# Turning the attention values around from the tile their projection writes, instead of from a copy that went through DRAM

## The chip, the core and the metric

The kernel runs on one core of a Trainium2 chip. The metric is the device time of one execution in microseconds (us); lower is better. A core has a matrix engine (TensorE, PE in the rows), a vector engine (VectorE, DVE), an activation engine (ScalarE, ACT), GpSimd (POOL) and SyncE (SP), which only issues transfers. Each engine works through its own list of instructions in order and waits on semaphores for the others. SBUF is the on-chip memory, PSUM the accumulators that TensorE writes.

## The reference, cut to what matters

One decoder layer over 1024 tokens of width 1024. All branches start from one projection of the normalised input:

```python
proj = h @ w_in
xa, za, q, k, v, zb, qi, ki, wi, ga, gb = jnp.split(proj, IN_SPLITS, axis=-1)
ya = s5_mixer(xa, ...)                       # state space branch, gated by za
yb = dsa_mixer(q, k, v, qi, ki, wi)          # 8 heads, one shared key/value head of width 64
merged = sigmoid(ga) * ya + sigmoid(gb) * (yb * silu(zb)) @ w_b_o
```

`dsa_mixer` scores all keys with an indexer, keeps 256 per query, and attends over them with softmax: `o = p @ v`, with `v` of 1024 x 64. To multiply by `v`, TensorE wants tokens on the partitions (the 128 rows of SBUF), while the projection delivers `v` with its 64 columns on the partitions and the tokens along the row. So `v` has to be transposed once.

## The kernel before

The kernel is one long program for a scheduling library: it says what depends on what and in which pool a tile lives, and the library fixes each engine's order and the semaphores. A pool of n buffers gives a new tile a buffer when the last user of an old one is done.

The projections are made in column blocks of 128 (`project`): the weights are loaded by SP, split into a high and a low part (ACT casts, DVE subtracts), and TensorE makes three products per pair of tiles (`three`, lines 137 to 139). The results go to PSUM banks that rotate among three (`dense_bank`) and are read out by ACT and DVE into tiles of the pool `stage`, which has three buffers of 128 x 1024 (`staged`). These three buffers serve many names one after the other: the raw values `vraw`, the gates `gas`, `gbs`, `zbs` on their way to DRAM, the eight blocks `wg` of the modulation weights that DVE sums into `gsum`, the query tile `qt0`, and the copy `vt` of the values.

In order of the program: the indexer's scores; the search for the top 256 (DVE counts); the state space branch (names `y`, `hs`, `mk`), woven together with the projections of q, k and v (`kv`), then of the gates `ga` (8 blocks), the first two blocks of `gb` and the four of `zb`. Then two products with `gsum` (`gate`, line 737), the transposes of `v` (line 754), and `flag_ps` (line 829), a 1 x 1 product that says whether the search succeeded. DVE casts it to an integer (`rows_ok`, line 831), loads it into a register and branches (line 833): with success it skips the slow exact search. Then attention begins: scores `l` (line 894), DVE adds the bias and finds the maximum (line 897), ACT takes the exponential (line 908), DVE divides (line 912), TensorE transposes (`pt`, line 919) and multiplies by `v_s` (lines 938 and 939). The remaining six `gb` blocks and other dense products are strewn between these by a table of numbers (`pace`, `leads`), so that TensorE has work while DVE and ACT make the softmax.

The values before: `with_v` copies rows 64 to 127 of the projection `kv` into `vraw`; ACT's queue stores them to `vd` in DRAM; much later SP loads `vd` into partitions 0 to 63 of a fresh staged tile `vt`, and TensorE transposes that in eight pieces into one PSUM bank, `v_ps`. `split` (lines 77 and 78) makes the high part of `v_s` on ACT and the low part on DVE. The PSUM pools of attention (`psl` and others) take over the banks that `ps_a.close()` gives back before the attention stage; the bank of `v_ps` and that of `flag_ps` are among them.

```python
def staged(name, dtype=F32, shape=(128, L)):
    return stage.tile(list(shape), dtype, name=name, tag="sg")
```

Of the kernel before, what the change touches and what calls it, by code (L numbers as in the profile page):

```python
# [9 lines left out]
F32 = mybir.dt.float32  # L10
F32R = mybir.dt.float32r
# [9 lines left out]
L = 1024  # L21
NT = L // 128
# [12 lines left out]
def tile_hybrid(ctx, tc, x, c, norm_g, w_mod, b_mod, w_in, a_re, a_im, b_re, b_im,  # L35
                c_re, c_im, d_skip, log_dt, w_glu, b_glu, w_a_o, w_b_o, w_out,
                final_g, out):
    nc = tc.nc
# [5 lines left out]
    def f32(ap):  # L44
        return ap.bitcast(F32)
# [8 lines left out]
    spill = ctx.enter_context(tc.tile_pool(name="spill", bufs=1, space=DRAM))  # L54

    def bank(name):
        return ps1.tile([128, 512], F32, name=name, tag="b1")
# [10 lines left out]
    ident = const.tile([128, 128], F32, name="ident")  # L68
# [4 lines left out]
    def staged(name, dtype=F32, shape=(128, L)):  # L73
        return stage.tile(list(shape), dtype, name=name, tag="sg")

    def split(src, hi, lo, hi_eng=None, lo_eng=None):
        (hi_eng or nc.scalar.copy)(hi, src)  # L77
        (lo_eng or nc.vector).tensor_sub(lo, src, f32(hi))  # L78
# [71 lines left out]
    def project(src, c0, m, rh, rl, nkt, name, early=True, pieces=(0, 1), rows=None):  # L150

        wh, wl = load_w(src, c0, m, nkt, name, early, rows)
        for j in pieces:
            sl = slice(512 * j, 512 * j + 512)
            ps = dense_bank(f"{name}_ps")
            for kt in range(nkt):
                three(ps[:m], wh[:, kt], wl[:, kt], rh[kt][:, sl], rl[kt][:, sl],
                      kt == 0, kt == nkt - 1)
            yield ps[:m], sl
# [2 lines left out]
    yds = []  # L162
    qd = spill.tile([8, 128, L], F32, name="qd")
    kd = spill.tile([2, 128, L], F32, name="kd")
    vd = spill.tile([64, L], F32, name="vd")
    zad = spill.tile([4, 128, L], F32, name="zad")
    zbd = spill.tile([4, 128, L], F32, name="zbd")
    gad = spill.tile([ND, 128, L], F32, name="gad")
# [5 lines left out]
    with ExitStack() as st:  # L174
# [32 lines left out]
        ps = bank("rows_ps")  # L207
# [92 lines left out]
    kpool = att.enter_context(tc.tile_pool(name="kpool", bufs=1, side="right"))  # L300
# [19 lines left out]
    def stack_k(parts, dst_h, dst_l, name):  # L320
        hi, lo = hi_lo(parts, name, 64)
        for o in (0, 64):
            nc.scalar.dma_start(f32(dst_h[o:o + 64]), hi[0:64])
            nc.scalar.dma_start(f32(dst_l[o:o + 64]), lo[0:64])
# [16 lines left out]
    with ExitStack() as st:  # L341
# [11 lines left out]
        for nm, src in (("ar", a_re), ("ai", a_im)):  # L353
# [4 lines left out]
            ps = bank(nm + "_ps")  # L358
# [100 lines left out]
        ps = bank("wi_ps")  # L459
# [5 lines left out]
        for i in groups[0] + groups[1]:  # L465
            w = 128 * (i + 1)
            for h in range(8):
                for o, n in chunks(w):
                    ps = bank(f"s{i}_{h}_{o}")
# [55 lines left out]
    for dst, e0, e1, nm in ((cx, c_re, c_im, "cxr"), (cy, c_im, c_re, "cyr")):  # L525
# [3 lines left out]
        ps = bank(nm + "_ps")  # L529
# [6 lines left out]
    ps = bank("dsk_ps")  # L536
# [47 lines left out]
    for m in range(4):  # L584
# [3 lines left out]
        for half in range(2):  # L588
# [23 lines left out]
            ps = bank(f"mt{q}_ps")  # L612
# [6 lines left out]
            ps = bank(f"k{q}_ps")  # L619
# [15 lines left out]
            ps = bank(f"s{q}_ps")  # L635
# [37 lines left out]
            ps = bank(f"y{q}_ps")  # L673
# [15 lines left out]
    ps = bank("rows2_ps")  # L689
# [6 lines left out]
    t = staged("vraw")  # L696

    def with_v(parts):
        for ps, sl in parts:
            nc.scalar.copy(t[64:128, sl], ps[64:128])  # L700
            yield ps, sl

    stack_k(with_v(project(w_in, K, 128, h_hi, h_lo, ND, "kv")), kd[0], kd[1], "k")
    nc.scalar.dma_start(vd, t[64:128])

    def gates(c0, ms, dst, silu, name):

# [11 lines left out]
    for kt in range(ND):  # L719
        t = staged(f"wg{kt}")  # L720
# [13 lines left out]
    for j in range(2):  # L734
        ps = bank(f"gate{j}")
# [10 lines left out]
    nc.sync.dma_start(f32(att_k), kd.rearrange("e p n -> p e n"))  # L746
    att_q = staged("qt0", F32R, (128, 8, 128))
    nc.sync.dma_start(f32(att_q), qd[:, :, 0:128].rearrange("h p n -> p h n"))
    att_v = kpool.tile([128, NT, 128], F32R, name="v_s")
    vt = staged("vt")  # L750
    nc.sync.dma_start(vt[0:64], vd)
    ps = bank("v_ps")
    for j in range(NT):
        nc.tensor.transpose(ps[:, 64 * j:64 * j + 64], vt[0:64, 128 * j:128 * j + 128], ident[:64, :64])
    split(ps.rearrange("p (j d) -> p j d", j=NT), att_v[:, :, 0:64], att_v[:, :, 64:128])


    for i in range(2):
# [5 lines left out]
    def scr(name, dtype=F32, n=6):  # L764
        return sepool.tile([128, n], dtype, name=name)
# [38 lines left out]
    for g, tiles in enumerate(groups):  # L804
        for n, i in enumerate(tiles):
# [7 lines left out]
            j = sepool.tile([128, L], F32, name=f"j{i}", tag="cf", bufs=2)[:, :w]  # L813
# [19 lines left out]
    with tc.If(found < 6 * 128):  # L833
# [4 lines left out]
        thr, d, cnt, need = scr("thr", I32), scr("d", I32), scr("cntb"), scr("need")  # L838
# [196 lines left out]
    for k, (m, pieces) in enumerate(steps):  # L1035
# [8 lines left out]
        t = wpool.tile([128, D], F32, name=f"wo{k}", tag="wraw")  # L1044
# [7 lines left out]
    for t in range(NT):  # L1052
# [6 lines left out]
        for n, (o, w) in enumerate(pieces):  # L1059
            sl = slice(o, o + w)  # L1060
            ps = pso.tile([128, 512], F32, name=f"o{t}_ps", tag="o")
# [48 lines left out]
```

## Time and profile before

| what | value |
|---|---|
| device time, median of 3 runs | 911.64 us (910.56 to 913.61) |
| time of the profiled execution | 913.2 us |
| its span, first to last instruction | 911.4 us |
| mean granted clock of TensorE | 0.975 of full |
| TensorE busy | 853.0 us, 94% of the span |
| VectorE busy | 655.6 us, 72% |
| ScalarE busy | 406.5 us, 45% |

The profiled execution is 1.8 us longer than its span; a change of the span is a change of the time. [...]

### The profile page before, as it was taken

How to read it: one execution, taken by the hardware profiler on the slowest of the kernel's cores; microseconds unless marked ns; L12 is line 12 of the kernel's file. 1: busy time of each engine (PE TensorE's matmuls, PEld its weight loads, DVE VectorE, ACT ScalarE, POOL GpSimd, SP SyncE). 2: the span in 40 equal slices, each digit the busy share in tenths (PEclk: the TensorE clock that was granted, in tenths of full speed). 3: DMA queues.
4: the chain of work that ended last, by engine and by line, in shares of the span. 5: the costliest groups of instructions: out<-in, count | busy, mean ns of one | idle time of the engine just before them, and what ended most of it. 6: DMA issues, size and time to landing. Idle time of an engine off the chain costs nothing.

```text
span 911.4 us, 12005 instructions
## 1 busy us (share of the span) xinstructions
PE 853.0 (94%) x4105; PEld 703.9 (77%) x4105; DVE 655.6 (72%) x1381; ACT 406.5 (45%) x803; POOL 138.2 (15%) x244
## 2 busy tenths in 40 slices
PE   4999999989889998999769999999999999999996
PEld 4887788877668877888558888887888888777885
DVE  5665898498989894687226677668987786956753
ACT  7553576354355542332225564457555443432311
POOL 0000100079446943000000000000000000221000
PEclk9799999999999998999969999999999999999999
DMA  9925611463443332573423323135314323644331
GB/s 328 315 65 131 147 49 47 74 181 89 121 117 119 110 111 65 183 263 92 116 70 97 92 83 112 47 105 151 103 47 129 92 81 93 198 150 149 139 131 54
DMA packets 124388, 110.38 MB, mean 121 GB/s; under 512 B 20954, under 2 KB 108066, under 8 KB 124324
## 3 DMA queue, kind: packets, MB, share of 16 engines
q1 hardware_dynamic: 96386, 77.46, 28.3%
q10 hardware_dynamic: 27938, 32.13, 12.0%
q8 instruction: 32, 0.52, 0.2%
q14 instruction: 32, 0.26, 0.1%
HBM read 76.67 MB, written 26.48 MB: 113 GB/s over the span
## 4 chain that ended last, share of the span: by engine, by line
PE 52%; DVE 13%; issue 4%; DMA 4%; ACT 2%; ACTq 2%; POOL 0%; DVEq 0%; SPq 0%
PE l L894 4%; DVE cj L770 3%; PE gb_ps L137 3%; PE gb_ps L138 3%; PE gb_ps L139 3%; PE pt L919 3%; PE o_ps L139 3%; PE o_ps L138 3%; PE o_ps L137 3%; PE pv L939 2%; PE pv L938 2%; PE ao_ps L139 2%; PE ao_ps L137 2%; PE ao_ps L138 2%; PE zb_ps L138 2%
## 5 line engine op out<-in xcount | busy, mean ns | idle before, releaser
L78 POOL TENSOR_TENSOR wo_l<-wo,wo_h 128x1024 fp32r<-128x1024 f32 x5 | 12.2, 2447 | 459.0 <-ACT wo_h L77 429.8
L770 DVE TENSOR_SCALAR_CACHE_REDUCE cj<-score,mid 128x1024 bf16<-128x1024 f32 (+2 forms) x72 | 67.6, 939 | 14.2 <-ACT mid L793 8.8
L897 DVE CUSTOM_DVE_ANT_0 S<-l,bias 128x384 f32<-128x384 f32 (+5 forms) x96 | 52.6, 553 | 26.5 <-PE l L894 23.4
L908 ACT ACTIVATE S<-S,stt 128x128 f32<-128x128 f32 (+7 forms) x64 | 49.1, 770 | 40.1 <-DVE stt L905 39.9
L77 ACT CAST ph<-pt 128x512 fp32r<-128x512 f32 x72 | 41.3, 584 | 43.4 <-PE pt L919 38.4
L78 DVE TENSOR_TENSOR pl<-pt,ph 128x512 fp32r<-128x512 f32 x72 | 48.8, 686 | 9.1 <-ACT ph L77 8.7
L894 PE MATMUL l<-k_s,qt 128*128 128x384 f32 (+5 forms) x192 | 50.2, 349 | 4.9 <-issue 4.9
L138 PE MATMUL gb_ps<-h_lo,gb_wh 128*128 128x512 f32 x128 | 51.4, 402 | 0.0
L137 PE MATMUL gb_ps<-h_hi,gb_wh 128*128 128x512 f32 x128 | 51.4, 401 | 0.0
L138 PE MATMUL o_ps<-wo_l,m_hi 128*128 128x512 f32 (+1 forms) x136 | 51.3, 378 | 0.0
L139 PE MATMUL o_ps<-wo_h,m_lo 128*128 128x512 f32 (+1 forms) x136 | 51.0, 377 | 0.1
L139 PE MATMUL gb_ps<-h_hi,gb_wl 128*128 128x512 f32 x128 | 51.1, 399 | 0.0
L139 PE MATMUL ga_ps<-h_hi,ga_wl 128*128 128x512 f32 x128 | 50.9, 397 | 0.0
L137 PE MATMUL ga_ps<-h_hi,ga_wh 128*128 128x512 f32 x128 | 50.7, 396 | 0.0
L138 PE MATMUL ga_ps<-h_lo,ga_wh 128*128 128x512 f32 x128 | 50.3, 393 | 0.0
L475 ACT ACTIVATE r<-s 128x512 f32<-128x512 f32 (+3 forms) x80 | 39.7, 525 | 23.2 <-PE s L471 15.4
L137 PE MATMUL o_ps<-wo_h,m_hi 128*128 128x512 f32 (+1 forms) x136 | 49.4, 377 | 0.2 <-ACT wo_h L77 0.2
L480 DVE SCALAR_TENSOR_TENSOR score<-r,wi_t,score 128x512 f32<-128x512 f32 (+3 forms) x70 | 42.1, 652 | 7.5 <-ACT r L475 6.6
L919 PE MATMUL pt<-ident,S 128*128 128x128 f32 x288 | 46.1, 272 | 0.0
L919 PEld LDWEIGHTS pt<-ident,S 128*128 128x128 f32 x288 | 36.5, 140 | 10.4
L471 PE MATMUL s<-ki_s,qi_s 128*128 128x384 f32 (+3 forms) x160 | 42.1, 355 | 1.8 <-DVE wi_t L464 1.3
L894 PEld LDWEIGHTS l<-k_s,qt 128*128 128x128 f32 x192 | 34.4, 191 | 10.4 <-issue 5.0
(402 smaller groups left out, 2400.7 us busy)
## 6 DMA issues: line engine op xcount, KB each, us to landing
wm<-in_w_mod_dram SPq DMA_DIRECT2D x16, 512.0 KB, 6.5
x_sb<-in_x_dram SPq DMA_DIRECT2D x8, 512.0 KB, 5.4
ga_w<-in_w_in_dram SPq DMA_DIRECT2D x8, 512.0 KB, 4.0
gad<-gas ACTq DMA_DIRECT2D x8, 512.0 KB, 2.6
gb_w<-in_w_in_dram SPq DMA_DIRECT2D x8, 512.0 KB, 4.4
wg<-in_w_mod_dram SPq DMA_DIRECT2D x8, 512.0 KB, 4.8
gbd<-gbs ACTq DMA_DIRECT2D x8, 512.0 KB, 3.1
qt<-qd SPq DMA_DIRECT2D x8, 512.0 KB, 4.0
```

Source lines behind the costliest of these rows:

```text
L77: (hi_eng or nc.scalar.copy)(hi, src)
L78: (lo_eng or nc.vector).tensor_sub(lo, src, f32(hi))
L137: paced(nc.tensor.matmul(ps, wh, rh, start=first, stop=False))
L138: paced(nc.tensor.matmul(ps, wh, rl, start=False, stop=False))
L139: mm = nc.tensor.matmul(ps, wl, rh, start=False, stop=last)
L471: mm = nc.tensor.matmul(ps[:, :n], qs[:, h, 128 * i:128 * i + 128], ks[:, e, o:o + n], start=e == 0, stop=e == 1)
L480: nc.vector.scalar_tensor_tensor(dst, r[:, :n], wi_t[:, i, h:h + 1], dst, op0=OP.mult, op1=OP.add)
L770: nc.vector.tensor_scalar(j, src, at, None, op0=op, op1=OP.add, accum_out=dst)
L894: mm = nc.tensor.matmul(ps[:, :n], qt[:, 4 * e2 + 2 * j + g], ks[:, e, o:o + n], start=e == 0, stop=e == 1)
L897: nc.vector.tensor_tensor_reduce(out=S[:, o:o + n], in0=ps[:, :n], in1=bias[i][:, o:o + n], scale=1.0, scalar=NEG, op0=OP.add, op1=OP.max, ...
L908: nc.scalar.activation(S2[j], S2[j], AF.Exp, scale=0.125, bias=nm[:, j:j + 1], accum_out=sm[:, j:j + 1])
L919: mm = nc.tensor.transpose(ps[:, 128 * j:128 * j + 128], Ss[i, g, j][:, 128 * kb:128 * kb + 128], ident)
```

## The change

The store of `vraw` to `vd` and the load of `vt` are taken out, and `vd` with them. The eight transposes read partitions 64 to 127 of `vraw` itself (with the matching corner of the identity), and they, their bank `v_ps` and the two halves of the split are written right behind the projection, ahead of the gates.

```diff
-    vd = spill.tile([64, L], F32, name="vd")
...
     stack_k(with_v(project(w_in, K, 128, h_hi, h_lo, ND, "kv")), kd[0], kd[1], "k")
-    nc.scalar.dma_start(vd, t[64:128])
+
+    att_v = kpool.tile([128, NT, 128], F32R, name="v_s")
+    ps = bank("v_ps")
+    for j in range(NT):
+        nc.tensor.transpose(ps[:, 64 * j:64 * j + 64], t[64:128, 128 * j:128 * j + 128], ident[64:128, 64:128])
+    split(ps.rearrange("p (j d) -> p j d", j=NT), att_v[:, :, 0:64], att_v[:, :, 64:128])
...
-    att_v = kpool.tile([128, NT, 128], F32R, name="v_s")
-    vt = staged("vt")
-    nc.sync.dma_start(vt[0:64], vd)
-    ps = bank("v_ps")
-    for j in range(NT):
-        nc.tensor.transpose(ps[:, 64 * j:64 * j + 64], vt[0:64, 128 * j:128 * j + 128], ident[:64, :64])
-    split(ps.rearrange("p (j d) -> p j d", j=NT), att_v[:, :, 0:64], att_v[:, :, 64:128])
```

Where this puts the instructions is decided by the library. TensorE's list at the passage to attention, before (`l` are the first scores, `gb` the dense filler):

```order
L139 MATMUL zb_ps<-h_hi_253,zb_wl 128x512
L737 MATMUL gate_3894<-gsum,ones 1x512
L737 MATMUL gate_3897<-gsum,ones 1x512
L754 MATMUL v_ps<-ident,vt 128x64 x8
L829 MATMUL flag_ps<-ones,sound 1x1
L833 UNCONDITIONAL_BRANCH
L894 MATMUL l_0_0_0_0_4958<-k_s,qt_3910 128x128 x2
L894 MATMUL l_0_0_1_0_4963<-k_s,qt_3910 128x128 x2
L137 MATMUL gb_ps<-h_hi_246,gb_wh 128x512
```

The same place in the changed program (lines from 703 to 748 are four higher there, lines from 753 on three lower):

```order
L139 MATMUL zb_ps<-h_hi_252,zb_wl 128x512
L741 MATMUL gate_3904<-gsum,ones 1x512
L741 MATMUL gate_3907<-gsum,ones 1x512
L826 MATMUL flag_ps<-ones,sound 1x1
L891 MATMUL l_0_0_0_0_4954<-k_s,qt_3920 128x128
L830 UNCONDITIONAL_BRANCH
L891 MATMUL l_0_0_0_0_4954<-k_s,qt_3920 128x128
L891 MATMUL l_0_0_1_0_4959<-k_s,qt_3920 128x128 x2
L137 MATMUL gb_ps<-h_hi_245,gb_wh 128x512
```

The transposes are gone from here, `flag_ps` follows the two `gate` products directly, and the first score product stands ahead of TensorE's own jump over the branch. The transposes have not gone to where they are written: a bank for `v_ps` comes free only when the state space branch returns its own, so they stand near the end of the `ga` products, behind `rows_ps`:

```order
L138 MATMUL ga_ps<-h_lo_258,ga_wh 128x512
L675 MATMUL y_ps<-u_2512,mk_1900 128x128
L689 MATMUL rows_ps<-ident,rows_2675 128x8
L707 MATMUL v_ps<-ident,vraw 128x64 x8
L139 MATMUL ga_ps<-h_hi_250,ga_wl 128x512
```

Until then `vraw` keeps one of the three staged buffers, which before was returned by the store. DVE's list at that place, before (`gsum` sums the `wg` blocks, `hs` is the state space branch, `j` and `best` are the search, `gb_wl` is a weight):

```order
L660 SCALAR_TENSOR_TENSOR hp_2652<-d_2642,sp_2637 128x512
L723 TENSOR_SCALAR gsum<-wg_3498,sc 128x1024
L815 SCALAR_TENSOR_TENSOR j_4290<-cj_h,score_718 128x1024
L665 TENSOR_TENSOR ha_2654<-hp_2652,ct_2339 128x512
L666 TENSOR_TENSOR hb_2655<-hp_2652,sn_t_2340 128x512
L692 COPY bg<-rows_ps 128x8
L816 MAX best<-j_4290 128x8
L671 TENSOR_TENSOR hs_2658<-ha_2654,hb_2655 64x2x127
```

And in the changed program:

```order
L671 TENSOR_TENSOR hs_2657<-ha_2653,hb_2654 64x2x127
L692 TENSOR_SCALAR bg<-bg 128x4
L78 TENSOR_TENSOR v_s<-v_ps,v_s 128x8x64
L727 TENSOR_SCALAR gsum<-wg_3508,sc 128x1024
L812 SCALAR_TENSOR_TENSOR j_4286<-cj_h,score_717 128x1024
L78 TENSOR_TENSOR gb_wl<-gb_w,gb_wh 128x1024
L729 SCALAR_TENSOR_TENSOR gsum<-wg_3511,sc,gsum 128x1024
L813 MAX best<-j_4286 128x8
```

The first sum into `gsum` stood ahead of `ha`, `hb` and the `hs`; now it stands behind them and behind the low half of `v_s`. On SP's list the eight loads of `wg` keep their place behind the first `zb` weight, but the first of them now takes the buffer of `gas6`, and the second that of `vraw`; before, the first found a buffer free.

## Rows read from the trace of the kernel before

**Rows 1.** The page's part 1: busy us (share of the span) and instructions.

```profile
PE 853.0 (94%) x4105; PEld 703.9 (77%) x4105; DVE 655.6 (72%) x1381; ACT 406.5 (45%) x803; POOL 138.2 (15%) x244
```

**Rows 2.** TensorE's waits from 466 us to the end: total, times, longest.

```profile
PE glb_ps L137 <- ACT yz_hi L77: 0.9, 1, 0.9
```

**Rows 3.** Timeline of 436 to 482 us: start, duration, instruction, [idle before, releaser].

```profile
447.56 1.88 PE L737 MATMUL gate<-gsum,ones 128*1 128x512 f32 x4
...
450.95 0.67 DVE L738 TENSOR_TENSOR bgate<-bgate,gate 1x512 f32<-1x512 f32 x1
451.05 0.33 ACTq L714 DMA_DIRECT2D zbd<-zbs  x1
...
456.17 0.52 SPq L751 DMA_DIRECT2D vt<-vd  x1
...
459.80 1.08 PE L754 MATMUL v_ps<-ident,vt 64*128 64x64 f32 x8 [10.37 <-DMA vt<-vd]
...
461.04 0.15 DVE L831 CAST rows_ok<-flag_ps 1x1 int32<-1x1 f32 x1 [9.42 <-PE flag_ps L829]
461.52 1.28 ACT L908 ACT_TABLE_LOAD   x1
...
465.12 0.69 DVE L78 TENSOR_TENSOR v_s<-v_ps,v_s 128x512 fp32r<-128x512 f32 x1 [3.93 <-DVEq L833]
...
465.91 1.09 PE L894 MATMUL l<-k_s,qt 128*128 128x128 f32 x4 [4.91 <-issue]
...
466.61 0.29 DVE L897 CUSTOM_DVE_ANT_0 S<-l,bias 128x128 f32<-128x128 f32 x1 [0.80 <-PE l L894]
...
468.70 0.48 DVE L912 TENSOR_SCALAR S<-S,stt 128x128 f32<-128x128 f32 x2
```

**Rows 4.** One-microsecond windows: length, busy (count) by engine, TensorE's clock, DMA share, GB/s.

```profile
452.00:453.00 1.00, 0.00 (x0) 0.00 (x0) 0.00 (x0) 0.71 (x1) 0.00 (x0) 1.00 0.65 125
453.00:454.00 1.00, 0.00 (x0) 0.00 (x0) 0.00 (x0) 0.00 (x0) 0.00 (x0) 0.56 1.03 276
...
470.00:471.00 1.00, 1.00 (x6) 0.83 (x5) 0.00 (x0) 0.00 (x0) 0.00 (x0) 0.91 0.87 237
```

**Rows 5.** TensorE's timeline at the second pair of transposes.

```profile
475.10 0.39 PE L139 MATMUL gb_ps<-h_hi,gb_wl 128*128 128x512 f32 x1
475.32 0.56 PE L894 MATMUL l<-k_s,qt 128*128 128x128 f32 x4
475.72 0.40 PE L919 MATMUL pt<-ident,S 128*128 128x128 f32 x2
```

**Rows 6.** Transfers of 460 to 466 us, the only queue with packets: packets, MB, share.

```profile
q14 instruction: 2, 0.02, 0.9%
```

**Rows 7.** ACT's timeline: the store of gas6 to DRAM is issued.

```profile
374.75 0.33 ACTq L714 DMA_DIRECT2D gad<-gas  x1
```

**Rows 8.** The page's part 6, the gas stores: KB each, us to landing.

```profile
gad<-gas ACTq DMA_DIRECT2D x8, 512.0 KB, 2.6
```

**Rows 9.** The tile wg: durations in ns, first and last start, time to landing.

```profile
L725 DVE SCALAR_TENSOR_TENSOR gsum<-wg,sc,gsum x7: 1265/1278/1286, 382.9 to 397.9; 128x1024 f32<-128x1024 f32 x7
L723 DVE TENSOR_SCALAR gsum<-wg,sc x1: 731/731/731, 376.9 to 376.9; 128x1024 f32<-128x1024 f32 x1
...
DMA to landing us min/median/max: 4.5/4.8/5.7
```

**Rows 10.** DVE's groups of 376.8 to 383 us: busy us, mean ns.

```profile
L671 DVE TENSOR_TENSOR hs<-ha,hb 64x254 f32<-64x254 f32 x2 | 0.8, 411 | 0.0
...
L665 DVE TENSOR_TENSOR ha<-hp,ct 128x512 f32<-128x512 f32 x1 | 0.7, 686 | 0.0
```

**Rows 11.** ACT and TensorE where block 1 of gb begins its second half.

```profile
397.19 1.09 ACT L711 ACTIVATE gbs<-gb_ps 128x512 f32<-128x512 f32 x2 [3.10 <-DVE gsum L725]
...
398.50 0.39 PE L137 MATMUL gb_ps<-h_hi,gb_wh 128*128 128x512 f32 x1
```

**Rows 12.** The window of 380 to 400 us, columns as in rows 4.

```profile
380.00:400.00 20.00, 20.00 (x97) 16.76 (x96) 19.58 (x27) 5.94 (x8) 0.00 (x0) 1.00 0.91 314
```

## The prediction

> **What bounds the kernel now.** I read the page's totals first: TensorE is busy for 94% of the span, the next engine for 72% [rows 1]. So time is lost where TensorE stands still, and the next views are its waits. From 466 us to the end they hardly exist: behind the wait that ends at 465.9 the longest is 0.9 us [rows 2]. Whatever brings that point of the program forward brings the end forward by as much, unless it opens a new wait.
>
> The passage to attention is the hole. In the timeline [rows 3] the reader is to see a chain. TensorE ends its `gate` products at 449.44 (447.56 + 1.88). DVE is done with them at 451.62 (450.95 + 0.67). The load of `vt` is issued only at 456.17, since it needs a staged buffer and waits for the store of `zbs`, issued at 451.05. TensorE gets its transposes at 459.80, after 10.37 us of waiting. `rows_ok` ends at 461.19. DVE's branch takes until 465.12 (3.93 us), then comes the low half of `v_s` until 465.81, and the first score product starts at 465.91. That wait is called "issue", but it ends 0.1 us after `v_s`, the last reader of the bank that the scores take over. On top, the clock falls: it is full up to 453 us, at half soon after [rows 4], 3.7 us after TensorE's last product, and comes back only near 470.2.
>
> **The change, step by step.** The sum is made on the profiled execution (span 911.4 us, time 913.2); that ran 1.6 us above the median of 911.64, so I take the change from the median.
>
> *Step 1, the wait for `vt` goes.* `flag_ps` now stands right behind `gate`. DVE reads it after its second `bgate` addition, at 451.62, and ends `rows_ok` 0.15 us later, near 451.75 instead of 461.19: 9.45 us earlier. What is late next is DVE, 2.3 us behind TensorE.
>
> *Step 2, the start of attention.* Before, 14.53 us pass from the end of `rows_ok` to the second pair of transposes at 475.72 [rows 3, 5]. I take that place because from there on TensorE runs through. In the changed program the last reader of the freed banks is `rows_ok`, ahead of the branch; so TensorE starts its scores 0.1 us after it and goes on with `gb` products while DVE branches. Two paths lead to the second pair:
> - DVE's: branch 3.93, then twice the way from the first `S` to the last division, 466.61 to 469.18 (468.70 + 0.48), 2.57 each, as the second pair's scores stand behind the first pair's divisions: 9.1 us.
> - TensorE's: eight score products at 0.1 us (four begin in 0.40 us [rows 5]), two transposes, 0.3, 27 `gb` products at the 0.22 to 0.23 us at which they follow each other at the full clock [rows 5], 6.1, and its own jump, which stands behind the first score product. On ACT the jump is hidden in the 0.6 us between `v_s` and the table load at 461.52, so up to 0.6. Together some 7.8.
>
> DVE's path decides: 9.1 instead of 14.5, 5.4 us gained. Bounds: if the clock falls all the same, TensorE's path is what it was from 465.91 to 475.72, 9.8, and with the jump 10.5 (gain 4.0); if the jump also costs 3.9 as DVE's does, 13.8 (gain 0.7). If DVE's branch cost nothing, TensorE's 7.8 would decide (gain 6.7). I take 5.4: TensorE would stand still for 2.3 us, less than the 3.7 after which the clock fell here.
>
> [...]
>
> *Step 3, the transposes move.* At half clock eight took 1.08 us [rows 3]; at the full clock near `rows_ps` I take half, 0.55 (between 0.5 and 1.08). TensorE runs through there, so it is paid. The halves of `v_s` hide on ACT, idle there, and on DVE are part of step 4. The store's issue on ACT and the transfers themselves were hidden; nothing for them.
>
> *Step 4, the staged buffer that `vraw` keeps.* For the `ga` blocks two buffers are enough: a store lands in 2.6 us [rows 8] and the next block's 48 products take 10.9. For `wg` it matters. Before, the first `wg` had a free buffer and its sum began at 376.9 [rows 9]; now it waits for the store of `gas6`, issued at 374.75 [rows 7], landed at 377.4, and needs 4.8 itself: 382.2. DVE is full here (19.58 of 20 us [rows 12]), and ACT reads the first half of `gb` block 0 only when the seventh sum gives back a buffer, at 397.19; TensorE needs that bank at 398.50 [rows 11]. The read takes 0.6, so 0.7 us are spare. From 376.9 to 397.1 DVE worked 20.2 us; of these `ha`, `hb`, four `hs` and small ones, 3.1 us [rows 10], now come ahead of the first sum, and 0.3 were idle: 16.8 remain. So 382.2 + 16.8 = 399.0; the later sums also wait for their own loads, which start later too, 0 to 3 (three turns of the buffers by the 0.9 between a usual and a slow landing), I take 0.8: 399.8, with the read 400.4. TensorE is there at 399.05 (0.55 later than before): it stands for 1.4 us, with the semaphore 1.5. Bounds: with the shortest landing, 4.5, and no other wait 0.2; with 5.7 and the whole 3, 4.4. Behind the waiting first sum stands the weight of `gb` block 1, done near 385.3 and needed near 393; on SP `k_s` moves back, which the scores need only after 450.
>
> Sum: 9.45 + 5.4 - 0.55 - 1.5 = 12.8 us; from the median 898.8, for a profiled run like this one 900.4. All bounds together: 15.4 (with 6.7, 0.5, 0.2) and 4.7 (with 0.7, 1.08, 4.4), so 896.2 to 906.9.
>
> **The rivals.**
> - *The wait re-forms at the branch.* TensorE's scores wait for something behind DVE's branch as before, and the clock falls. For it: the old wait ended behind the branch. Against: only the low half of `v_s` stood there, and it has left. Then step 2 saves only `v_s`, 0.7: 9.45 + 0.7 - 2.05 = 8.1 us, 903.5.
> - *DVE's branch gets longer.* The two packets in the branch's window are instructions [rows 6], and all else was quiet; in the changed program the store of `zbs`, issued at 451.05 and in by 456.17, moves during the branch. If the branch's 3.93 us counted only from there, it would end 4.4 us later than from 451.75; I price the middle, 2.2: 10.6 us, 901.0. [...]
> - *Slower: `wg` is starved.* If `wg` really had one buffer, each of its blocks would take load and sum, 4.8 + 1.28 = 6.1 us [rows 9]; the seventh sum would end at 377.4 + 42.6 = 420.0, and TensorE, there at 399.05, would stand for 21.6 us: 12.8 + 1.5 - 21.6, or 7.3 us slower, 918.9. It decides from a seventh sum after about 413. Against it: the second load takes `vraw`'s buffer right behind the transposes near 379.5.
> - *No gain.* The query tile or another load holds the scores until attention begins as late as before. `qt0` was issued at 444.6 and would have to take 20 us; every other one in these views lands within 6.
>
> **How the numbers follow.** My case has 70%, with a range of its own from the sum's best to 901.5; the longer branch 12%, the re-formed wait 10%, starved loads 4%, no gain 4%. The time is 898.8. The range reaches from 896 to 903.5: it holds my case, the branch and half of the re-formed wait. About 0.3%, 2.7 us, can be told from no change here. My case, the branch and the re-formed wait are faster, 0.92; no gain is the same, 0.04; starved loads are slower, 0.04.
>
> **What would show it.** Step 1: `rows_ok` right behind the second `bgate`, TensorE's wait there near 2.3 us. Step 2: first scores 0.1 us after `rows_ok`, the clock staying at 1.0, the second pair of transposes 9.1 us after it, with a wait of TensorE for DVE of about a microsecond. Step 3: eight transposes near 379 us in 0.55. Step 4: a new wait of TensorE for ACT's `gbs` near 399 us, 1.5 us long, and the first `gsum` near 382. A wait of TensorE over 4 us at either place would make the prediction wrong, as would a clock that falls at 453.

## The result and the profile after

| | before | changed |
|---|---|---|
| median of the runs of one comparison, us | 912.62 (910.56 to 914.98, 6 runs) | 905.70 (902.94 to 907.80, 6 runs) |
| ratio to before, 95% interval | | 0.9911 (0.9892 to 0.9931) |
| span of the profiled execution, us | 911.4 | 903.2 |

The change makes the kernel faster by 0.9%: by the ratio 8.1 us, with an interval of 6.3 to 9.9. That is the sign that was forecast and too little of it: 898.8 was predicted, with a range up to 903.5.

To see where the profiled pair parts, I cut both spans into the same five stretches by four marks of TensorE. The tile view gives two of the marks, the first product of `gb` and of `zb` (the second number of a row is the start of the last one). Before:

```profile
L137 PE MATMUL gb_ps<-h_hi,gb_wh x128: 387/389/735, 380.5 to 560.3; 128*128 128x512 f32 x128
L137 PE MATMUL zb_ps<-h_hi,zb_wh x64: 389/389/389, 403.9 to 446.8; 128*128 128x512 f32 x64
```

The changed kernel, the same two rows:

```profile
L137 PE MATMUL gb_ps<-h_hi,gb_wh x128: 387/391/628, 380.1 to 551.8; 128*128 128x512 f32 x128
L137 PE MATMUL zb_ps<-h_hi,zb_wh x64: 389/389/389, 407.4 to 450.2; 128*128 128x512 f32 x64
```

| stretch of TensorE | before, us | changed, us | gain |
|---|---|---|---|
| start to the first `gb` product | 380.5 | 380.1 | 0.4 |
| first `gb` to first `zb` product | 23.4 | 27.3 | -3.9 |
| first `zb` product to the `gate` products | 43.7 | 43.6 | 0.1 |
| `gate` products to the second pair of transposes | 28.2 | 16.1 | 12.0 |
| from there to the end of the span | 435.7 | 436.1 | -0.4 |

The sum is 8.2, the difference of the spans. (In the kernels below, whose programs are nearly the same up to there, the first `gb` product starts anywhere from 377 to 384 us, and in one of them at 390; so stretches are compared, not places.) Two rows hold what matters: the passage to attention gave 12.0 us where 14.85 was forecast (9.45 + 5.4), and the stretch around 399 us took back 3.9.

The passage of the changed kernel, as in [rows 3] (start, duration, instruction, [idle before, releaser]):

```profile
451.02 1.88 PE L741 MATMUL gate<-gsum,ones 128*1 128x512 f32 x4
...
453.91 0.37 SPq L115 DMA_DIRECT2D gb_w<-in_w_in_dram  x1
454.41 0.67 DVE L742 TENSOR_TENSOR bgate<-bgate,gate 1x512 f32<-1x512 f32 x1
454.51 0.33 ACTq L718 DMA_DIRECT2D zbd<-zbs  x1
455.01 0.14 DVE L828 CAST rows_ok<-flag_ps 1x1 int32<-1x1 f32 x1
...
455.25 0.63 PE L891 MATMUL l<-k_s,qt 128*128 128x128 f32 x4 [2.33 <-issue]
...
460.76 0.29 DVE L894 CUSTOM_DVE_ANT_0 S<-l,bias 128x128 f32<-128x128 f32 x1 [5.61 <-DVEq L830]
...
460.98 0.28 DVE L894 CUSTOM_DVE_ANT_0 S<-l,bias 128x128 f32<-128x128 f32 x1
...
463.12 0.08 DVE L894 DVE_READ_ACCUMULATOR2_ANT stt<- 128x1 f32 x1 [1.86 <-issue]
...
464.55 0.48 DVE L909 TENSOR_SCALAR S<-S,stt 128x128 f32<-128x128 f32 x2
...
467.15 0.52 PE L916 MATMUL pt<-ident,S 128*128 128x128 f32 x2 [0.18 <-DVE S L909]
```

`rows_ok` stands right behind the second `bgate`, and the first scores start 0.10 us after its end, as forecast. But DVE comes out of its branch 5.61 us after `rows_ok`, not 3.93, and then stands still once more for 1.86 us between its second score row and reading its maximum, waiting for nothing that the profile shows. So the first `S` to the last division takes 4.27 us (460.76 to 465.03) instead of 2.57, and the second pair of transposes comes 12.0 us after `rows_ok`.

Around 399 us, in the changed kernel, ACT's and TensorE's timelines:

```profile
397.80 0.39 PE L139 MATMUL gb_ps<-h_hi,gb_wl 128*128 128x512 f32 x1
...
399.56 1.09 ACT L715 ACTIVATE gbs<-gb_ps 128x512 f32<-128x512 f32 x2 [4.68 <-DVE gsum L729]
...
400.21 0.50 PE L137 MATMUL gb_ps<-h_hi,gb_wh 128*128 128x512 f32 x1 [2.02 <-ACT gbs L715]
```

and its one-microsecond windows, columns as in [rows 4]:

```profile
400.00:401.00 1.00, 0.79 (x3) 0.67 (x4) 1.00 (x2) 0.65 (x2) 0.00 (x0) 1.00 1.11 327
401.00:402.00 1.00, 1.00 (x4) 0.82 (x3) 0.96 (x4) 0.34 (x1) 0.00 (x0) 0.62 0.90 320
402.00:403.00 1.00, 1.00 (x4) 0.71 (x4) 0.97 (x2) 0.26 (x1) 0.00 (x0) 0.50 0.78 315
403.00:404.00 1.00, 1.00 (x4) 0.81 (x3) 0.71 (x1) 0.26 (x1) 0.00 (x0) 0.50 0.00 0
404.00:405.00 1.00, 1.00 (x5) 0.78 (x4) 0.39 (x1) 0.58 (x1) 0.00 (x0) 0.68 0.00 0
```

The forecast wait for `gbs` is there, 2.02 us. What was not forecast stands behind it: TensorE is already at work again when its clock falls from 1.00 to 0.50 (the third-last column), for about 3.4 us if the 0.62 and the 0.68 at the ends are time at either of these two values, which 886 of the first 900 one-microsecond windows of this profile show. In these 3.4 us a product starts every 0.43 us instead of every 0.23. (A count in a window takes in the products that only reach into it.) Wait and half clock are nearly all of the 3.9 us. The first sum into `gsum` was not where it was forecast, as the tile view of `wg` shows, with DVE's idle time before its sums (us, times):

```profile
L727 DVE TENSOR_SCALAR gsum<-wg,sc x1: 747/747/747, 380.4 to 380.4; 128x1024 f32<-128x1024 f32 x1
...
  DMA wg<-in_w_mod_dram: 2.1, 2
```

### The profile page after: what moved, and what is told of

Its sections match the earlier page's. It is cut to its first block, busy times and chain, and to the rows that moved or that the text cites. A ratio compares the mean times of both kernels' runs of the same rounds, so it can differ in the third digit from the quotient of the medians.

```text
span 903.2 us, 12003 instructions
## 1 busy us (share of the span) xinstructions
PE 854.9 (95%) x4105; PEld 704.1 (78%) x4105; DVE 655.7 (73%) x1381; ACT 406.5 (45%) x803; POOL 138.4 (15%) x244
```

## The experiments

All are compared with the kernel before, in runs beside it on one chip.

### The start of attention

*Without the branch.* The conditional block is left out, and with it the exact search, which is not entered with these inputs:

```
     nc.vector.tensor_copy(rows_ok[0:1], flag[0:1, 0:1])
-    found = nc.vector.value_load(rows_ok[0:1, 0:1])
-    with tc.If(found < 6 * 128):
...
```

> The changed kernel without the conditional block behind rows_ok: the exact search that it holds is left out (it is not entered with these inputs). My theory: DVE's way over the branch and the code that it then has to fetch set the start of attention. Then DVE's first score row S starts 0.6 to 1.0 us after rows_ok instead of 5.6, and the second pair of transposes comes 9.3 to 9.8 us after rows_ok instead of 12.0, by TensorE's own work (27 products, 7 of them at half clock); the end 2.2 to 2.7 us earlier, near 903.3. Rival, the half clock of TensorE sets it: the second pair stays within 0.5 us of 12.0.

Measured: 900.06 us, ratio 0.9853 (0.9819 to 0.9886). Its timeline:

```profile
454.93 0.14 DVE L828 CAST rows_ok<-flag_ps 1x1 int32<-1x1 f32 x1
...
455.62 0.29 DVE L862 CUSTOM_DVE_ANT_0 S<-l,bias 128x128 f32<-128x128 f32 x1 [0.55 <-PE l L859]
...
462.95 0.40 PE L884 MATMUL pt<-ident,S 128*128 128x128 f32 x2
```

DVE starts 0.55 us after `rows_ok`, its second stall is gone too, and the second pair comes 7.9 us after `rows_ok` instead of 12.0. I had put it at 9.3 to 9.8, with a half clock that did not come this time. So the branch with the block behind it holds up this passage by about 4 us (12.0 less 7.9). The end came 5.3 us before the changed kernel's by the ratios, where 2.2 to 2.7 were expected.

*Quiet while DVE branches.* Two transfers are put off: the store of the last `zb` block behind the first exponentials on ACT, one weight load behind the second query load on SP.

```
+            if f"{name}{m}" == "gb5": first.append(qtd[1])
...
-            nc.scalar.dma_start(dst[m], t)
+            late.append(nc.scalar.dma_start(dst[m], t))
...
+                if (i, g, e2) == (0, 0, 0): order(late[13], late[-1])
```

> The changed kernel with two transfers put off until DVE is over its branch: the store of the last zb block stands behind the first two exponentials on ACT, the load of the weight of gb block 5 behind the second query load on SP. My theory: DVE's branch took 5.6 us instead of 3.9 since its code had to be fetched while these 1 MB were under way. Then it takes 3.8 to 4.2, its first instruction packet starts about 1.9 us after rows_ok instead of 3.4, and the end comes 1.3 to 1.8 us earlier, near 904.1. Rival: the branch takes 5.4 to 5.8 us without the traffic too, and the time stays.

Measured: 902.92 us, ratio 0.9893 (0.9858 to 0.9928), which by time alone is not to be told from the changed kernel's. The timeline tells it:

```profile
453.12 0.14 DVE L829 CAST rows_ok<-flag_ps 1x1 int32<-1x1 f32 x1
...
457.08 0.29 DVE L895 CUSTOM_DVE_ANT_0 S<-l,bias 128x128 f32<-128x128 f32 x1 [3.82 <-DVEq L831]
...
459.25 0.08 DVE L895 DVE_READ_ACCUMULATOR2_ANT stt<- 128x1 f32 x1 [1.67 <-issue]
...
463.28 0.52 PE L918 MATMUL pt<-ident,S 128*128 128x128 f32 x2 [0.18 <-DVE S L910]
```

The branch is back at 3.82 us, the figure of before, and the second pair comes 10.0 us after `rows_ok`. The second stall stays, 1.67 us. The load of `rows_ok` into DVE's register, in the tile view (duration in ns three times over, start), is part of the branch. Changed kernel:

```profile
L829 DVEq TENSOR_LOAD <-rows_ok x1: 1487/1487/1487, 455.2 to 455.2; - x1
```

Quiet kernel:

```profile
L830 DVEq TENSOR_LOAD <-rows_ok x1: 542/542/542, 453.4 to 453.4; - x1
```

What else the profile shows in this time is packets of the queue that it names instruction (instruction packets below). In quarter-microsecond windows of the transfers they lie in two of the windows from `rows_ok` to the end of the second stall (packets, MB, share). Changed kernel, at 458.5 and at 461.0:

```profile
q14 instruction: 1, 0.01, 7.7%
...
q14 instruction: 1, 0.01, 14.7%
```

The quiet kernel has its two at 454.85 and 457.35. In both, DVE goes on about 2.2 us after the first packet, and the second stall ends some 2 us after the second one, which comes about 2.5 us after the first. The profile does not say for which engine a packet is, nor what it brings; that DVE goes on 2.1 to 2.3 us after the first one's window begins in all eight profiles with the branch at this place speaks for DVE, and that it brings the code behind the branch is my reading. The time from the end of the register load to the first packet differs as well: 0.9 us when quiet (453.94 to 454.85), 1.8 with the two transfers under way (456.69 to 458.5), each to a quarter of a microsecond.

*The other direction*: the kernel before with extra loads while DVE branches.

```
-    nc.sync.dma_start(vt[0:64], vd)
+    nc.sync.dma_start(vt[0:64], vd); [nc.sync.dma_start(vt[64:128], w_mod[64 * n:64 * n + 64, 0:1024]) for n in range(6)]
```

> The kernel before with six extra loads of 256 KB into the unused half of vt, two of them on SP ahead of the branch, so that transfers are under way while DVE branches, which was quiet before (3.93 us). My theory: the code behind the branch is fetched over the same transfer engines, so the branch takes over 4.8 us, with its first instruction packet over 2.5 us after rows_ok. Rival: it takes 3.8 to 4.1 us as before.

One run, 910.93 us. Its branch took 4.42 us:

```profile
462.53 0.69 DVE L78 TENSOR_TENSOR v_s<-v_ps,v_s 128x512 fp32r<-128x512 f32 x1 [4.42 <-DVEq L833]
```

Longer than 3.93, but it lies between what the two theories gave, and its register load took 0.54 us as in a quiet kernel: the last extra load ahead of the branch was issued at 457.66, and it is a quarter of what is under way in the changed kernel. Its first instruction packet came 2.1 us after `rows_ok`, not over 2.5. And in the kernel that only holds the buffer (below), whose passage is as quiet as before's, the branch took 4.12 us:

```profile
465.98 0.69 DVE L78 TENSOR_TENSOR v_s<-v_ps,v_s 128x512 fp32r<-128x512 f32 x1 [4.12 <-DVEq L833]
```

The run decides nothing.

*Is it the clock?* The changed kernel once more, in another comparison:

> The changed kernel once more, beside the two rearrangements on one chip, to see how much its profile varies from run to run: both theories expect 903 to 908 us, a wait for gbs of 2 to 3 us near 399, DVE's branch between 5 and 6 us with the two transfers under way, and a stall of DVE of 1.5 to 2 us behind its second score row.

Measured: 905.20 us, ratio 0.9910 (0.9878 to 0.9943). Its branch took 5.56 us, the second stall 1.70 and its wait for `gbs` 2.5. Its windows, where in the first profile of the same kernel the clock was at half from 456 to 459 us:

```profile
456.00:457.00 1.00, 1.00 (x7) 0.81 (x7) 0.00 (x0) 0.68 (x2) 0.00 (x0) 1.00 0.80 215
457.00:458.00 1.00, 1.00 (x6) 0.83 (x5) 0.00 (x0) 1.00 (x1) 0.00 (x0) 1.00 1.09 307
...
460.00:461.00 1.00, 0.00 (x0) 0.00 (x0) 0.02 (x1) 0.00 (x0) 0.00 (x0) 1.00 0.00 0
...
462.00:463.00 1.00, 1.00 (x4) 0.48 (x2) 0.00 (x0) 0.00 (x0) 0.00 (x0) 0.50 0.64 155
```

Up to 459 us, at the full clock, TensorE was merely done sooner with its products and waited for DVE; behind this wait the clock fell here too, from 462.0 to 465.4:

```profile
461.33 0.44 PE L891 MATMUL l<-k_s,qt 128*128 128x128 f32 x2 [1.89 <-DVE stt L894]
...
467.29 0.44 PE L916 MATMUL pt<-ident,S 128*128 128x128 f32 x2
```

The second pair came 11.9 us after `rows_ok` (end 455.43), against 12.0 in the first profile. So the branch and the second stall take nearly the same wherever the half clock lies. That the clock costs this stretch nothing is not shown by this pair alone, since both profiles have some 3.4 us at half; the kernel with the earlier bank, below, says more on it.

### The stretch around 399 us

*Only the held buffer.* The kernel before, plus one transpose that nobody reads; it keeps `vraw`'s staged buffer as long as the changed kernel does, and gives SP and DVE the changed kernel's order there.

```
-    nc.scalar.dma_start(vd, t[64:128])
+    nc.scalar.dma_start(vd, t[64:128]); nc.tensor.transpose(bank("hold_ps")[:, 0:64], t[64:128, 0:128], ident[64:128, 64:128])
```

> The kernel before, plus one small transpose of the raw tile at the place where the changed kernel has its eight: its result is read by nobody, it only keeps the staged buffer of vraw until the S5 stage is done. My theory: this alone makes the chain of wg late. Then the first sum moves from 376.9 to about 380, TensorE waits 2 to 3 us for gbs, the clock falls behind that wait, and from the first gb product to the first zb product 27 to 28 us pass instead of 23.4; the end comes 3.5 to 4.5 us later than before, near 916.5. Rival, the held buffer is not what delays the gate products: less than 1 us.

Measured: 916.69 us against 913.65, ratio 1.0043 (1.0026 to 1.0060), that is 3.9 us by the ratio, 2.4 to 5.5. Its waits of TensorE (total, times, longest), of which the second is new against before:

```profile
PE v_ps L754 <- DMA vt<-vd: 10.2, 1, 10.2
...
PE gb_ps L137 <- ACT gbs L711: 1.6, 1, 1.6
```

and its two marks:

```profile
L137 PE MATMUL gb_ps<-h_hi,gb_wh x128: 387/389/735, 379.5 to 561.3; 128*128 128x512 f32 x128
L137 PE MATMUL zb_ps<-h_hi,zb_wh x64: 389/389/389, 404.8 to 447.6; 128*128 128x512 f32 x64
```

So the held buffer alone makes the kernel slower, by the wait that was forecast. In this profile the stretch took 25.3 us, not the 27 to 28 that I expected: the wait was 1.6 us and the clock stayed up behind it. The profiled execution was the fastest of the ten (914.0 us); where the other 2 us of the median lie is not shown.

*An earlier bank for the transposes*, so that the buffer comes free sooner.

```
-    ps = bank("v_ps")
+    ps = dense_bank("v_ps")
```

> The transposes of the values write a bank of the projections instead of one of the S5 stage, so they need not wait for that stage and the staged buffer of vraw comes free some 15 us earlier. My theory: the wait of TensorE for gbs (2.0 us) and the half clock behind it (about 1.5 us) both come from the held buffer, so both vanish: the first sum starts near 377 us, the last read of the first gb block near 397, and the end comes 3 to 3.5 us earlier than in the changed kernel, near 902.3. Rival: the gate products come 3.4 us late for another reason (the order of the S5 stage, the transposes themselves): then less than 1 us is won.

Measured: 910.35 us, ratio 0.9961 (0.9938 to 0.9984): by the medians 4.7 us slower than the changed kernel where 3 to 3.5 less were expected. The wait for `gbs` shrank to 0.5 us, but the scheduler moved the state space branch with the transposes, and TensorE came to its first `gb` product at 390.2 us. One edit moved too much; it says nothing on the theory of the held buffer. It does say something on the start of attention:

```profile
468.27 0.29 DVE L894 CUSTOM_DVE_ANT_0 S<-l,bias 128x128 f32<-128x128 f32 x1 [5.54 <-DVEq L830]
...
468.70 0.08 DVE L894 DVE_READ_ACCUMULATOR2_ANT stt<- 128x1 f32 x1
...
472.86 0.41 PE L916 MATMUL pt<-ident,S 128*128 128x128 f32 x2
```

With the same two transfers under way the branch took 5.54 us, the clock was at half from 463.8 to 467.2, and a second instruction packet came 2.5 us after the first; but DVE did not stand still for it, and the second pair came 10.1 us after `rows_ok` (end 462.73). DVE's own way makes up the 10.1 (5.54 and twice 2.3). So here the half clock under the branch costs nothing, the second stall is what the changed kernel's 12.0 has beyond it, about 1.9, and a branch need not bring one.

### What the trip through DRAM costs

*The kernel before with an earlier load.* Store and load of the values stay; only `vt` is staged and loaded ahead of the last `zb` block.

```
+    vt = staged("vt")
+    nc.sync.dma_start(vt[0:64], vd)
     dense[:] = 0, 1
     gates(ZB, (3,), zbd, True, "zb")
...
-    vt = staged("vt")
-    nc.sync.dma_start(vt[0:64], vd)
```

> The kernel before, with the store and the load of the values kept; only the staged tile vt and its load stand ahead of the last zb block instead of behind the gate products. My theory: the wait was for the staged buffer, not for the trip through DRAM. Then the 10.4 us wait of the transposes vanishes, rows_ok ends about 3.5 us behind the gate products, and the time is within 2 us of the changed kernel's (the gbs wait near 399 us is absent, but the low half of v_s and the scores stand behind the branch). Rival, the gain came from the scores that start ahead of the branch: then it stays over 4 us slower than the changed kernel.

Measured: 902.97 us, ratio 0.9876 (0.9838 to 0.9914), level with the changed kernel or ahead of it. The 10.4 us were the wait for a staged buffer, and an earlier place in the queue removes it as well as the change does. It has no wait for `gbs` (first `gb` 383.8 to first `zb` 407.2: 23.4 us), but the first query tile now came late, and the start of attention took 13.7 us from `rows_ok` (454.94) to the second pair (468.59):

```profile
458.16 1.09 PE L894 MATMUL l<-k_s,qt 128*128 128x128 f32 x4 [4.72 <-DMA qt<-qd]
...
461.82 0.29 DVE L897 CUSTOM_DVE_ANT_0 S<-l,bias 128x128 f32<-128x128 f32 x1 [6.28 <-DVEq L833]
```

Transfers ran through this branch too, up to 460.3 us, and it is the longest of all, 6.28 us, with a second stall of 2.10 behind it.

### A version that beats both

*Branch, flag and gate products ahead of the last `zb` block*, in the changed kernel:

```
     gates(ZB, range(3), zbd, True, "zb")
-    dense[:] = 0, 1
-    gates(ZB, (3,), zbd, True, "zb")
-    s5.close()
-    for j in range(2):
-        ps = bank(f"gate{j}")
...
     found = nc.vector.value_load(rows_ok[0:1, 0:1])
     with tc.If(found < 6 * 128):
...
+    for j in range(2):
+        ps = bank(f"gate{j}")
...
+    dense[:] = 0, 1
+    gates(ZB, (3,), zbd, True, "zb")
+    s5.close()
```

> The changed kernel with the exact search's branch, the flag and the gate products ahead of the last zb block in program order, so that DVE branches while TensorE still has over ten microseconds of products. My theory: DVE's branch and the fetch of the code behind it are then hidden, TensorE does not wait for rows_ok, and from the last zb product to the second pair of transposes 7.5 to 9 us pass instead of 16.1 (1.9 of it are the gate products, which only move): 5 to 6.5 us less, near 900. Rival, the start of attention is bound by TensorE's own work and its clock: less than 2 us.

Measured: 904.45 us, ratio 0.9901 (0.9874 to 0.9927): hardly anything. DVE's branch was hidden, but SP had the first query tile behind loads that wait for the branch, and a new wait of TensorE took the place of the old:

```profile
PE l L891 <- DMA qt<-qd: 3.6, 1, 3.6
```

The same on the kernel before, with `vt` and the query tile ahead of the last `zb` block:

> The kernel before (values stored and loaded) with the branch, flag and gate products ahead of the last zb block, and with vt and the first query tile staged there too. My theory: it has neither the held buffer (the 3.9 us around 399 us) nor the wait for vt nor DVE's branch on the path, so it ends some 3 to 4 us ahead of the same rearrangement of the changed kernel, near 896. Rival, removing the trip through DRAM is what counts: then it ends behind it.

902.50 us, ratio 0.9875 (0.9842 to 0.9908), where 896 was expected: again a new wait, 2.9 us for the low half of `v_s`. So both were mended: the query tile (and in the kernel before `vt` and its transposes) two blocks ahead.

```
-    gates(ZB, range(3), zbd, True, "zb")
+    gates(ZB, range(2), zbd, True, "zb")
+    att_q = staged("qt0", F32R, (128, 8, 128))
+    nc.sync.dma_start(f32(att_q), qd[:, :, 0:128].rearrange("h p n -> p h n"))
+    gates(ZB, (2,), zbd, True, "zb")
```

On the changed kernel:

> The rearrangement of the run before (branch, flag and gate products ahead of the last zb block), built on the changed kernel, with the first query tile loaded ahead of it too, since there TensorE waited 3.6 us for that tile. My theory: what keeps attention from starting is now neither a transfer nor DVE's branch, so from the last zb product to the second pair of transposes under 10 us pass instead of 16.1, and TensorE has no wait over 1 us there; the wait for gbs near 399 us stays. The end 4 to 6 us ahead of the changed kernel, near 900. Rival: a further wait takes the place (the scores' banks, DVE's sums of zb), and less than 2 us are won.

Measured: 897.85 us, ratio 0.9822 (0.9786 to 0.9858), with the wait for `gbs` at 3.9 us and no wait of TensorE at the passage. On the kernel before:

> The same rearrangement built on the kernel before, with the store and the load of the values kept, and with vt, its transposes and the first query tile ahead of the last two zb blocks. My theory: besides the early start of attention it lacks the held buffer, so from the first gb product to the first zb product 23 to 24 us pass; the end 2 to 4 us ahead of the same rearrangement of the changed kernel, near 897. Rival, the trip through DRAM costs something by itself: level with it or behind.

Measured: 896.00 us, ratio 0.9807 (0.9779 to 0.9835). The two are not to be told apart by time; by place they are: from the first `gb` to the first `zb` product this one takes 23.4 us (381.6 to 405.0), the other 30.2 (380.1 to 410.3). The passage of this one:

```profile
444.28 0.68 DVE L855 TENSOR_TENSOR bgate<-bgate,gate 1x512 f32<-1x512 f32 x1 [2.21 <-DVEq L820]
...
451.30 0.39 PE L139 MATMUL zb_ps<-h_hi,zb_wl 128*128 128x512 f32 x1
451.52 0.56 PE L895 MATMUL l<-k_s,qt 128*128 128x128 f32 x4
...
459.19 0.41 PE L920 MATMUL pt<-ident,S 128*128 128x128 f32 x2
```

DVE branches under the last `zb` products, and the scores follow these without a gap.

## Why the prediction was wrong

*Step 1* was right: from the end of the `gate` products to the end of `rows_ok` 2.25 us pass (452.90 to 455.15), 2.3 was forecast. The earlier load shows that the wait was for the buffer, as the step said, and not for the trip.

*Step 2* is the step that failed, by 2.9 us (12.0 instead of 9.1). "DVE's: branch 3.93, then twice the way from the first `S` to the last division" took a duration from a quiet stretch into a busy one, and took it for the whole price. The branch in the changed kernel shares the time with 1 MB of transfers and takes 5.61; with these put off it takes 3.82 again. The first way from `S` to the last division took 4.27, the second 2.12, since its first `S` starts under that division: 5.61 + 4.27 + 2.12 = 12.0. The 4.27 hold a second stall that no row of before showed as a wait, 1.7 to 1.9 us in the changed and the quiet kernel. I put it down to the second instruction packet, an estimate from its place 2.1 and 1.9 us ahead of the stall's end; before, that packet came at 465.5, under `v_s`, and no stall is seen behind it. The rival "DVE's branch gets longer" had the transfers under way, with which the 1.7 us between 3.93 and 5.61 came and went; it priced them at 2.2, and had not the second stall. That the branch itself waits for a transfer of code is not shown by any run; what the eight profiles show is DVE going on 2.1 to 2.3 us after the first instruction packet. That the clock would stay at 1.0 was wrong in both profiles of the changed kernel (at half from 455.8 to 459.3 in the first, from 462.0 to 465.4 in the second); in the first it fell behind the wait of 2.33 us, although that is less than the 3.7 of before, where every window from 454 to 470 us has 0.50.

*Step 3* was right: the transposes took 0.64 us of TensorE (377.73 to 378.37), 0.55 was forecast:

```profile
377.73 0.71 PE L707 MATMUL v_ps<-ident,vraw 64*128 64x64 f32 x8
```

*Step 4* had the mechanism and too small a price. ACT read `gb` block 0 at 399.56 (forecast 399.8), TensorE waited 2.02 us (forecast 1.5), as it was there at 398.2 and not at 399.05. That ACT's time fits so well is partly luck: the first sum came at 380.35 instead of 382.2, its load having landed while DVE was still at `hs` and `v_s`, and DVE then waited 2.05 us for later loads where 0.8 was put. And the term left out that TensorE's clock fell to 0.50 behind this wait. The half clock cost another 1.6: eight products at 0.43 instead of 0.23 us. With the mark at 380 us, which came 0.4 earlier, steps 3 and 4 took 3.5 us instead of 2.05.

Sum: 12.8 forecast, less 2.8 in the passage, less 1.45 here, less 0.4 behind it, is the 8.2 of the profiled pair. Of the rivals, the starved loads and "no gain" did not happen; the re-formed wait has the measured gain, 8.1 us, by luck, since the scores did start ahead of the branch. That the branch and the second stall cause the shortfall in the passage is shown by the kernels without the branch, with the transfers put off and with the earlier bank; that the longer branch is due to the transfers rests on one profile with them put off, and on branches of 3.8 to 4.1 us in three quiet passages against 5.5 to 6.3 in four busy ones. That the held buffer causes the wait for `gbs` is shown by the kernel that only holds it. The half clock behind that wait stands in the windows of the changed kernel's first profile and in those of the quiet kernel (0.50 from 399 to 401 us); no run takes away the clock alone. Why the clock falls behind one wait of 2.3 us and not behind another of the same length stays open, and so does why the second stall is there in one program and not in another.

## What to carry to other kernels

Price a branch by a row that shows it (here DVE went on 3.8 to 6.3 us after `rows_ok`, 0.54 to 1.49 of them the register load), and ask what else is moving at that time; then look for work, or an earlier place, that covers it. When a tile is kept longer in a rotating set of buffers, follow the next users of that set to the engine that waits, and ask what the clock may do behind the wait that comes of it: here it cost 1.6 us behind one of 2.02. And before a store and a load are taken out, try an earlier place for the load: here it gave as much without holding the buffer.

## What was unexpected of the hardware

- A branch on DVE cost 3.8 to 4.1 us when nothing else moved (three profiles), 4.42 with a quarter of a megabyte and 5.5 to 6.3 with 1 to 1.5 MB under way (four); the register load in it took 0.54 us in the three quiet ones and the one with a quarter of a megabyte, and 1.01, 1.23 and 1.49 in three of the busy ones.
- Behind the branch a second instruction packet came 2.5 to 2.75 us after the first in all eight of these profiles, and DVE stood still for 1.7 to 2.1 us in four of them; in the one with the earlier bank it did not.
- TensorE's clock stayed at 1.00 behind a wait for `gbs` of 1.6 us (the kernel that only holds the buffer). It fell to 0.50 behind the one of 2.02 us in the first profile of the changed kernel, only after TensorE had been at work again for about 1 us, and in the quiet kernel at the end of a standstill of at least 2.5 us at that place (396.0 to 398.5; 0.56 in the window from 398). With the waits of 2.5 us (the changed kernel again) and 3.9 (its rearrangement) the stretch took 1.9 and 2.9 us beyond the wait and the 23.4 of before, with that of 1.6 only 0.3. Behind the 2.33 us wait for `rows_ok` the clock fell in two of five profiles (the first of the changed kernel and the one with the earlier bank); in the second one of the changed kernel it fell only behind the next wait, of 1.89 us for DVE.
